# Two hybrid layers on one core: gate steps traced behind the recurrence, and the scheduler's other model of times

## The chip, the cores and the metric

One core of a Trainium2 chip runs the whole program. The metric is the device time of one execution in microseconds (us), the median of several runs. The profile is of one execution more.

## What is computed

Two consecutive layers of a diffusion backbone on 256 context tokens and 256 latent tokens of width 1024. In each layer, cut to what matters:

```
u   = modulate(x)                              # adaLN, one shift and scale per stream
z   = u @ w_in                                 # one combined projection
ys  = [rwkv7(z0), retnet(z1), hgrn2(z2), gqa(z3)]   # four mixers, 256 columns each
m   = sum_i sigmoid(u @ w_gate_i) * (ys[i] @ w_branch_i)
x   = layer_norm(alpha * x + gate1 * (m @ w_out))
x   = layer_norm(alpha * x + gate2 * moe(modulate(x)))   # 16 experts, each picks its tokens, SwiGLU
```

The output is the latent stream after the second layer; layer 1 therefore computes only the 256 latent rows behind its mixers. All is in float32; a product with a weight is made of three products of halves (high x high, high x low, low x high), for which every weight is split into a rounded part and a rest.

## The kernel before

Weights stream from memory once. A layer runs in this order: modulation, input projection, attention, HGRN, RetNet, the RWKV recurrence, the gates, the output projection, the router, and the experts.

**The gates.** For three of the four branches (`wmg`, merged with the branch's weight) there are 8 steps each. A step loads a tile `wr` of 128 x 1280 on SP's queue (`wload`, L238), splits it into `wh` (ScalarE, L183) and `wl` (L211; for all steps of layer 0 and nearly all of layer 1 on POOL, else on VectorE), runs 24 products with u and, after a `yield`, 6 products with the branch's output. For the fourth branch, whose y is RWKV's own output, 8 steps `wg0` run 24 products each (names `m<-mh,wh`, `m<-mh,wl`, `m<-ml,wh` in layer 0, `yh`, `yl`, `y` for `mh`, `ml` in parts of layer 1); `merge_last` (L1325) then makes its 48 branch products. Columns are 512 in layer 0, 256 in layer 1. Buffers of `wr` are 4 in layer 0 and 3 in layer 1, of `wh` and `wl` 2.

**What sets the order.** The program is traced in Python; a list scheduler then walks it with a model of each instruction's time, and gives a free engine the ready instruction that was traced first. So what is traced early has a high priority. `merge_steps` (L1278) is a generator, kept as `self.filler`, and `hook(name)` (L403) traces as many of its half steps as the table `FILL` gives for that place. The recurrence (`rwkv`, L469, with `rwkv_early`, `rwkv_inverse`, `rwkv_late`) calls `hook` after each of its pieces; the keys of these are like `0X0`, `0inv0`, `1W1`, `1f`. Keys that begin with `hl` behind the layer's number, `0hf` and `1hf`, and `1fm` are for other generators (`mods`, `ret_proj`), in attention, HGRN and RetNet. What is left of the generator is traced by `fill()` (L410, called at L1908 in `layer`), behind the recurrence and behind x1, `wout`, `g2` and the router's rows:

```
        self.filler = self.merge_steps(l, lo, u, mg, mgp, yp, ys)
        self.rwkv(l, lo, ys[0], freed)
...
        nc.sync.dma_start(x1, src.rearrange("(t p) d -> p t d", p=P)[:, t0:])
...
        self.fill()
        mh, ml = self.merge_last(l, lo, mg, mgp, ys[0], xs.tile([P, 2, NTOK - lo], F32R, tag="oht", name="yl", bufs=1))
```

**The queues.** SP issues nearly all loads, in the scheduler's order, and each waits at the head of the queue until its buffer is free. When the recurrence's pool is freed by its last product, the loads of x1, `wrt`, `ring` and `first` (experts' weights in 1 MB units) may go; two tiles `rows_in` of `wout` go on POOL's queue (L1893). An expert takes 12 units of 1 MB (`w_e1`, `w_e3`, `w_e2`, four each); the units rotate through the buffers `ring`, `mid`, `low` and `late` (L1548), and the next unit of a buffer can be loaded when PE has read the last one.

Of the kernel before, what the change touches and what calls it, by code (L numbers as in the profile page):

```python
# [50 lines left out]
C_N = C_EVEN + 2  # L51


FILL = {
# [6 lines left out]
}  # L61


def shape_constants():
# [102 lines left out]
class Block:  # L167
# [235 lines left out]
    def hook(self, name):  # L403

        n = FILL.get(f"{self.l}{name}", FILL.get(name, 0))
        work = self.proj if name.startswith("hl") else self.filler
# [1578 lines left out]
```

## Time and profile before

| | us |
|---|---|
| median of 3 runs | 2302.59 |
| lowest, highest | 2302.35, 2312.79 |
| the profiled execution | 2311.96 |
| its span | 2310.2 |
| PE busy in it (89%) | 2048.9 |
| VectorE busy (45%) | 1041.0 |
| ScalarE busy (27%) | 627.2 |
| POOL busy (12%) | 268.1 |

The mean granted clock of the tensor engine is 0.929 of full speed. PE is busy nearly all the time in the mixers of both layers, and the DMA engines nearly all the time among the experts. Of the chain of waits that ended last, PE's work is 63%, transfers 22% and VectorE 10%.

### The profile page before, as it was taken

To read this page: it belongs to the slowest core of one execution; us is meant where nothing else is said; L and a number is where in the kernel's file an instruction comes from. 1 tells how busy PE (TensorE), PEld (TensorE's weight loads), DVE (VectorE), ACT (ScalarE), POOL (GpSimd) and SP (SyncE) were. 2 spreads that over 40 slices of the span, in tenths; PEclk is the share of its full clock that TensorE was granted. 3 is DMA by queue.
4 is the path that set the end of the run, shared out by engine and by line. 5 is a ranking of instruction groups with operands and counts; after the bars stand their busy time and mean duration, and the time that the engine had idled before them with its cause. 6 is when DMAs were issued, how large, how long until landed. Compare 5 with 4: busy or idle time off the path is not lost.

```text
span 2310.2 us, 37585 instructions
## 1 busy us (share of the span) xinstructions
PE 2048.9 (89%) x15964; PEld 1275.7 (55%) x15964; DVE 1041.0 (45%) x2179; ACT 627.2 (27%) x1039; POOL 268.1 (12%) x190
## 2 busy tenths in 40 slices
PE   6999999999999989999999899999889888766775
PEld 3657847677877744333332555868889654222222
DVE  3557755855532536222222557848664642010112
ACT  3353435422222212000000444555343320000000
POOL 2000111233332000000000200103353000000000
PEclk8999999999999989999999899998899988787777
DMA  8354242112124588999999646214222899999996
GB/s 317 97 194 155 64 142 73 41 58 70 56 66 184 201 351 326 422 425 425 426 426 425 220 138 211 69 47 165 92 93 86 338 372 424 424 425 423 424 425 288
DMA packets 96936, 554.85 MB, mean 240 GB/s; under 512 B 11296, under 2 KB 13280, under 8 KB 46848
## 3 DMA queue, kind: packets, MB, share of 16 engines
q1 hardware_dynamic: 95024, 541.83, 60.1%
q0 software_dynamic: 1200, 8.52, 0.9%
q8 instruction: 125, 2.05, 0.3%
q10 hardware_dynamic: 544, 2.10, 0.2%
q14 instruction: 43, 0.35, 0.0%
HBM read 549.13 MB, written 3.28 MB: 239 GB/s over the span
## 4 chain that ended last, share of the span: by engine, by line
PE 63%; DMA 22%; DVE 10%; ACT 2%; issue 2%; POOL 1%; SPq 0%; DVEq 0%; ACTq 0%; POOLq 0%
PE pj L201 14%; PE m L201 13%; PE h L201 12%; PE y L201 9%; DMA late<-in_w_e_dram 8%; PE g L201 6%; DMA mid<-in_w_e_dram 4%; DMA ring<-in_w_e_dram 4%; DMA pair<-in_w_e_dram 3%; PE mod L201 3%; PE w L201 3%; DMA mw<-in_wmod_dram 1%; DMA y<-in_wmod_dram 1%; DVE kb L186 1%; PE w L206 1%
## 5 line engine op out<-in xcount | busy, mean ns | idle before, releaser
L211 POOL TENSOR_TENSOR wl<-wr,wh 128x1280 fp32r<-128x1280 f32 (+1 forms) x62 | 177.7, 2867 | 292.6 <-ACT wh L183 266.2
L183 ACT ACTIVATE wh<-wr 128x1024 fp32r<-128x1024 f32 (+1 forms) x126 | 143.4, 1139 | 190.0 <-PE pj L201 86.4
L201 PE MATMUL m<-mh,wh 128*128 128x512 f32 (+1 forms) x512 | 183.4, 358 | 7.7 <-ACT th L183 7.7
L201 PE MATMUL m<-mh,wl 128*128 128x512 f32 (+1 forms) x512 | 179.4, 350 | 1.0 <-POOL wl L211 1.0
L201 PE MATMUL m<-ml,wh 128*128 128x512 f32 (+1 forms) x512 | 179.0, 350 | 0.0
L201 PE MATMUL h<-late,later 128*32 128x256 f32 (+1 forms) x880 | 143.1, 561 | 28.5 <-DMA late<-in_w_e_dram 28.5
L196 DVE SCALAR_TENSOR_TENSOR h<-h 128x512 f32<-128x512 f32 (+1 forms) x32 | 17.7, 555 | 313.9 <-ACT h L183 313.9
L211 DVE TENSOR_TENSOR wl<-wr,wh 128x1024 fp32r<-128x1024 f32 (+1 forms) x64 | 79.2, 1240 | 109.3 <-ACT wh L183 104.6
L183 ACT ACTIVATE h<-h 128x512 f32<-128x512 f32 (+1 forms) x32 | 15.7, 491 | 401.8 <-PE h L201 401.8
L201 PEld LDWEIGHTS m<-mh,wh 128*128 128x128 f32 x512 | 101.0, 197 | 25.7 <-ACT th L183 9.4
L186 DVE TENSOR_TENSOR h<-h 128x512 f32<-128x512 f32 (+1 forms) x32 | 17.7, 554 | 211.3 <-PE h L201 211.3
L201 PE MATMUL h<-ring,later 128*32 128x256 f32 (+1 forms) x640 | 93.6, 540 | 19.9 <-DMA ring<-in_w_e_dram 19.9
L201 PEld LDWEIGHTS m<-mh,wl 128*128 128x128 f32 x512 | 100.6, 196 | 13.8 <-issue 1.7
L201 PEld LDWEIGHTS h<-late,later 128*32 128x32 f32 (+1 forms) x880 | 45.5, 138 | 112.6 <-issue 63.4
L201 PEld LDWEIGHTS m<-ml,wh 128*128 128x128 f32 x512 | 100.8, 197 | 11.5 <-issue 1.6
L183 ACT ACTIVATE ht<-w 128x512 f32<-128x512 f32 (+1 forms) x32 | 15.7, 491 | 277.4 <-PE w L206 277.4
L201 PE MATMUL y<-late,ht 128*32 128x256 f32 (+1 forms) x536 | 73.5, 501 | 9.5 <-DMA late<-in_w_e_dram 6.9
L201 PE MATMUL h<-mid,later 128*64 128x512 f32 (+1 forms) x352 | 65.6, 569 | 9.0 <-DMA mid<-in_w_e_dram 9.0
L201 PEld LDWEIGHTS h<-ring,later 128*32 128x32 f32 (+1 forms) x640 | 30.1, 136 | 74.1 <-DMA ring<-in_w_e_dram 33.5
L201 PE MATMUL y<-ring,ht 128*32 128x256 f32 (+1 forms) x448 | 62.3, 526 | 9.7 <-DMA ring<-in_w_e_dram 6.3
L183 ACT ACTIVATE th<-m 128x512 f32<-128x512 f32 (+1 forms) x50 | 24.6, 492 | 164.6 <-PE m L201 164.6
L201 PE MATMUL pj<-mh,wl 128*128 128x512 f32 x152 | 61.9, 407 | 0.0
(629 smaller groups left out, 4480.5 us busy)
## 6 DMA issues: line engine op xcount, KB each, us to landing
late<-in_w_e_dram SPq DMA_DIRECT2D x144, 1024.0 KB, 19.5
ring<-in_w_e_dram SPq DMA_DIRECT2D x109, 1024.0 KB, 19.7
mid<-in_w_e_dram SPq DMA_DIRECT2D x63, 1024.0 KB, 19.7
pair<-in_w_e_dram SPq DMA_DIRECT2D x36, 1024.0 KB, 19.6
wr<-in_wmg_dram SPq DMA_DIRECT2D x48, 640.0 KB, 3.9
mw<-in_wmod_dram SPq DMA_DIRECT2D x48, 512.0 KB, 5.0
y<-in_wmod_dram SPq DMA_DIRECT2D x48, 512.0 KB, 4.0
low<-in_w_e_dram SPq DMA_DIRECT2D x20, 1024.0 KB, 19.8
```

Source lines behind the costliest of these rows:

```text
L183: self.nc.scalar.activation(out=out, in_=in_, func=func, **kw)
L186: self.nc.vector.tensor_tensor(out, a, b, op)
L196: self.nc.vector.scalar_tensor_tensor(out, a, s, b, op0, op1)
L201: self.nc.tensor.matmul(out, lhsT, rhs, start=start, stop=stop)
L206: self.nc.tensor.transpose(out, in_, self.ident[b:b + n, b:b + n])
L211: (eng or self.nc.vector).tensor_tensor(lo, src, hi.bitcast(F32), ALU.subtract)
```

## The change

Two edits. The table loses every key of the recurrence's hooks, so that `hook` traces no gate there and all 32 steps of a layer are traced by `fill()`, with the lowest priority of what can run then. And the tile context schedules with its other model of times. No instruction and no arithmetic is added or removed. Behind the table the changed kernel's line numbers are lower by 7.

```diff
-FILL = {
-    "0hf": 2, "0X0": 2, "0inv0": 1, "0W0": 3, "0R0": 3, "0Y0": 2, "0X1": 1, "0inv1": 1, "0W1": 2, "0R1":
...
+FILL = {'0hf': 2, '0hl00': 1, '0hl02': 1, '0hl04': 1, '0hl10': 3, '0hl12': 2, '0hl16': 1, '1hf': 2, '1hl00': 1, '1hl04': 1, '1hl06': 1, '1hl12': 1, '1hl16': 3, '1hl18': 3, '1hl11': 1, '1fm': 1, '0hl18': 2, '1hl15': 1, '1hl13': 1}
...
-    with tile.TileContext(nc) as tc:
+    with tile.TileContext(nc, schedule_with_timeline_sim=True) as tc:
```

On PE, runs of 24 to 96 gate products stood in the recurrence of layer 0 at the hooked places, and 186 products (merge_last's 48 among them) behind the router's product `wrr`. Now many short runs stand in the recurrence, 90 products between the transposes of `rx` and `wrr` (44 before), and 390 behind it. In layer 1 the last run grows from 62 to 240. The second HGRN scan of layer 0 has 54 projection products of 512 columns between its steps, where 86 stood.

POOL in layer 0, from the recurrence's second half to the gates' end (`wl` is a split, `ktm` and `tmp` belong to the recurrence, `y` is its last sum, `rows_in` is `wout`). Before:

```order
L703 MEMSET tmp 128x256
L704 MEMSET tmp 128x16
L211 TENSOR_TENSOR wl<-wr,wh 128x1280 x7
L646 TENSOR_TENSOR kb_3579<-kb_3579,ec 128x512 x2
L211 TENSOR_TENSOR wl<-wr,wh 128x1280
L764 MEMSET ktm 32x16x32 x2
L211 TENSOR_TENSOR wl<-wr,wh 128x1280 x8
L211 TENSOR_TENSOR wl<-wr,wh 128x1024 x2
L551 TENSOR_TENSOR y_114<-y_114,bo_5791 128x512
L551 TENSOR_TENSOR y_114<-y_114,bo_5799 128x512
L1893 DMA rows_in<-in_wout_dram 128x2048 x2
L211 TENSOR_TENSOR wl<-wr,wh 128x1024 x6
```

The same piece with the change:

```order
L696 MEMSET tmp 128x256
L697 MEMSET tmp 128x16
L204 TENSOR_TENSOR wl<-wr,wh 128x1280 x3
L639 TENSOR_TENSOR kb_3454<-kb_3454,ec 128x512 x2
L204 TENSOR_TENSOR wl<-wr,wh 128x1280
L757 MEMSET ktm 32x16x32 x2
L204 TENSOR_TENSOR wl<-wr,wh 128x1280 x8
L544 TENSOR_TENSOR y_114<-y_114,bo_4811 128x512
L544 TENSOR_TENSOR y_114<-y_114,bo_4819 128x512
L1886 DMA rows_in<-in_wout_dram 128x2048 x2
L204 TENSOR_TENSOR wl<-wr,wh 128x1280 x6
L204 TENSOR_TENSOR wl<-wr,wh 128x1024 x8
```

Behind the recurrence's last sum 6 splits stood, and now 14; in layer 1 it was 1, and is 10. Of the 62 splits on POOL 38 are left ahead of these sums.

SP in layer 1, at the end of the gates (`wg` are the g0 steps, `wb` the last branch's weight). Before:

```order
L242 DMA wr<-in_wmg_dram 128x1280 x24
L242 DMA wr<-in_wg_dram 128x1024 x7
L530 DMA g_14065<-in_g_dram 128x256
L242 DMA wr<-in_wg_dram 128x1024
L242 DMA wr<-in_wb_dram 128x1024 x2
L1896 DMA x_14196<-xd 128x2x1024
L1904 DMA wrt<-in_wrt_dram 128x128
L1569 DMA ring_14766<-in_w_e_dram 128x2048
L1569 DMA ring_14768<-in_w_e_dram 128x2048
L1569 DMA ring_14770<-in_w_e_dram 128x2048
L1569 DMA first<-in_w_e_dram 128x2048 x3
```

The same piece with the change:

```order
L235 DMA wr<-in_wmg_dram 128x1280 x4
L235 DMA wr<-in_wg_dram 128x1024
L1889 DMA x_13046<-xd 128x2x1024
L1897 DMA wrt<-in_wrt_dram 128x128
L1562 DMA ring_14766<-in_w_e_dram 128x2048
L1562 DMA ring_14768<-in_w_e_dram 128x2048
L1562 DMA ring_14770<-in_w_e_dram 128x2048
L235 DMA wr<-in_wg_dram 128x1024
L1562 DMA first<-in_w_e_dram 128x2048 x3
L235 DMA wr<-in_wg_dram 128x1024 x6
L235 DMA wr<-in_wb_dram 128x1024 x2
```

Seven of the eight loads of g0 weights have moved behind x, and six of them behind the first expert units too. In layer 0 the last two of the 24 `wmg` loads and all eight of g0 stand behind x, two rings and first.

SP among the experts of layer 0, some 18 units after the first reload. Before:

```order
L1569 DMA late_7270<-in_w_e_dram 128x2048
L1569 DMA late_7272<-in_w_e_dram 128x2048
L1569 DMA ring_7274<-in_w_e_dram 128x2048
L1569 DMA ring_7276<-in_w_e_dram 128x2048
L1569 DMA ring_7278<-in_w_e_dram 128x2048
L1569 DMA mid_7280<-in_w_e_dram 128x2048
L1569 DMA mid_7282<-in_w_e_dram 128x2048
L1569 DMA mid_7284<-in_w_e_dram 128x2048
L1569 DMA mid_7286<-in_w_e_dram 128x2048
L1569 DMA low_7288<-in_w_e_dram 128x2048
L1569 DMA late_7290<-in_w_e_dram 128x2048
```

The same piece with the change:

```order
L1562 DMA late_7270<-in_w_e_dram 128x2048
L1562 DMA mid_7280<-in_w_e_dram 128x2048
L1562 DMA mid_7282<-in_w_e_dram 128x2048
L1562 DMA mid_7284<-in_w_e_dram 128x2048
L1562 DMA mid_7286<-in_w_e_dram 128x2048
L1562 DMA low_7288<-in_w_e_dram 128x2048
L1562 DMA late_7290<-in_w_e_dram 128x2048
L1562 DMA late_7272<-in_w_e_dram 128x2048
L1562 DMA ring_7274<-in_w_e_dram 128x2048
L1562 DMA ring_7276<-in_w_e_dram 128x2048
L1562 DMA ring_7278<-in_w_e_dram 128x2048
```

Six units that were behind a late and three ring units have gone ahead of them. Such exchanges go on for some five experts of layer 0 and for three of layer 1; the order behind them is the old one.

## Rows read from the trace of the kernel before

**Rows 1.** Page, slices: GB/s moved in 40 equal slices of the span.

```profile
GB/s 317 97 194 155 64 142 73 41 58 70 56 66 184 201 351 326 422 425 425 426 426 425 220 138 211 69 47 165 92 93 86 338 372 424 424 425 423 424 425 288
```

**Rows 2.** Windows, recurrence of layer 0: engines busy (instructions), PE clock, DMA share, GB/s.

```profile
430.00:480.00 50.00, 45.45 (x563) 35.36 (x561) 37.82 (x85) 22.22 (x40) 13.35 (x6) 1.00 0.17 54
480.00:560.00 80.00, 79.29 (x925) 65.13 (x929) 36.77 (x50) 17.18 (x20) 25.95 (x11) 0.98 0.21 67
560.00:640.00 80.00, 76.62 (x1048) 63.11 (x1040) 46.85 (x79) 23.64 (x33) 23.98 (x11) 0.98 0.17 56
640.00:700.00 60.00, 58.31 (x458) 41.68 (x453) 20.13 (x34) 21.19 (x29) 17.44 (x9) 1.00 0.30 104
```

**Rows 3.** Windows, layer 1's recurrence, the same columns.

```profile
1570.00:1600.00 30.00, 25.76 (x250) 22.12 (x249) 27.12 (x61) 14.53 (x30) 12.77 (x9) 0.83 0.57 227
1600.00:1660.00 60.00, 53.19 (x782) 47.79 (x783) 45.04 (x100) 26.07 (x47) 22.45 (x12) 0.88 0.26 88
1660.00:1700.00 40.00, 36.52 (x582) 33.25 (x583) 32.52 (x66) 10.68 (x17) 11.41 (x5) 0.92 0.16 51
1700.00:1760.00 60.00, 56.84 (x1046) 54.09 (x1044) 29.34 (x47) 20.06 (x30) 29.84 (x12) 1.00 0.31 101
```

**Rows 4.** Timeline of PE, end of layer 0's gates: start, us, instruction, idle before.

```profile
691.37 1.98 PE L201 MATMUL w<-rows,ident 128*128 128x512 f32 x4 [1.69 <-ACT g L183]
...
699.75 0.39 PE L201 MATMUL m<-ml,wh 128*128 128x512 f32 x1
699.98 0.39 PE L201 MATMUL m<-mh,wl 128*128 128x512 f32 x1
704.35 0.66 PE L201 MATMUL w<-wrr,one 128*128 128x64 f32 x2 [3.98 <-DVE wrr L1443]
...
705.34 0.63 PE L201 MATMUL m<-ml,wh 128*128 128x512 f32 x1
705.77 0.63 PE L201 MATMUL m<-mh,wl 128*128 128x512 f32 x1
```

**Rows 5.** Timeline of PE, layer 1: gate products, and their end.

```profile
1753.57 0.28 PE L201 MATMUL m<-yh,wl 128*128 128x256 f32 x1
1753.68 0.28 PE L201 MATMUL m<-yh,wh 128*128 128x256 f32 x1
...
1796.37 2.93 PE L201 MATMUL w<-rows,ident 128*128 128x512 f32 x3 [2.48 <-ACT g L183]
```

**Rows 6.** Timeline of SP's queue: x1 in layer 0 and in layer 1.

```profile
688.70 0.38 SPq L1896 DMA_DIRECT2D x<-in_xt_dram  x1
...
1790.92 0.39 SPq L1896 DMA_DIRECT2D x<-xd  x1
```

**Rows 7.** Timeline of VectorE: an ordinary operation, and three that meet a split.

```profile
394.09 3.05 DVE L186 TENSOR_TENSOR z<-zp 128x512 f32<-128x512 f32 x1 [3.46 <-ACT zp L183]
...
438.22 0.22 DVE L186 TENSOR_TENSOR tmp<-tmp 128x60 f32<-128x60 f32 x1
...
439.21 2.37 DVE L186 TENSOR_TENSOR tmp<-tmp 128x63 f32<-128x63 f32 x1
...
1791.20 4.40 DVE L186 TENSOR_TENSOR y<-y,gt 128x256 f32<-128x256 f32 x2 [2.98 <-POOL y L551]
```

**Rows 8.** Timeline of POOL: one of the splits.

```profile
438.50 3.01 POOL L211 TENSOR_TENSOR wl<-wr,wh 128x1280 fp32r<-128x1280 f32 x1 [9.58 <-ACT wh L183]
```

**Rows 9.** Windows, HGRN and RetNet of layer 0, columns as in rows 2.

```profile
215.00:375.00 160.00, 155.80 (x928) 108.27 (x928) 100.41 (x222) 71.96 (x112) 18.28 (x23) 1.00 0.27 85
```

**Rows 10.** Windows, the experts of layer 0, columns as in rows 2.

```profile
834.00:870.00 36.00, 35.23 (x166) 12.42 (x163) 4.18 (x8) 3.59 (x8) 0.00 (x0) 1.00 0.94 373
870.00:900.00 30.00, 30.00 (x168) 18.12 (x166) 25.96 (x52) 10.63 (x23) 0.00 (x0) 1.00 0.75 286
900.00:940.00 40.00, 38.44 (x177) 13.44 (x178) 10.98 (x22) 2.10 (x4) 0.00 (x0) 1.00 0.97 381
...
1000.00:1250.00 250.00, 235.86 (x1060) 81.58 (x1062) 66.46 (x127) 16.63 (x28) 0.12 (x1) 1.00 1.01 425
```

More of the change, by code (lines that the diff above doesn't have):

```diff
@@ L51 @@
 C_N = C_EVEN + 2
-FILL = {
[6 rows of a table removed]
-}
+FILL = {'0hf': 2, '0hl00': 1, '0hl02': 1, '0hl04': 1, '0hl10': 3, '0hl12': 2, '0hl16': 1, '1hf': 2, '1hl00': 1, '1hl04': 1, '1hl06': 1, '1hl12': 1, '1hl16': 3, '1hl18': 3, '1hl11': 1, '1fm': 1, '0hl18': 2, '1hl15': 1, '1hl13': 1}
 def shape_constants():
```

5 rows, old and new, of the table FILL are left out of this document.

## The prediction

> **What bounds the kernel now.** I read the utilisation slices first, then busy time by stretch, the timelines of the places that the order moves, and at last the two streams of loads. The slices show two regimes in each layer. From about the 17th slice (920 us) to the 22nd, and from the 34th to the last but one, the DMA engines move 422 to 426 GB/s; these are the experts, and the loads alone set their length [rows 1]. In the other slices the transfers run far below that, and PE does the work of the mixers and the gates. So a change of order can gain in three ways only: PE waits less among the mixers, PE gets more of its clock there, or the experts' loads start or run with fewer holes.
>
> Layer 0, 430 to 700 us, is the RWKV recurrence with gates around it. PE is busy 45.45, 79.29, 76.62 and 58.31 of 50, 80, 80 and 60 us [rows 2], which leaves 10.3 us of waits, with a granted clock of 0.98 to 1.0. The same stage of layer 1, 1570 to 1760 us, has busy times of 25.76, 53.19, 36.52 and 56.84 in 30, 60, 40 and 60 us, so 17.7 us of waits, and clocks of 0.83, 0.88, 0.92 and 1.00 [rows 3]. If the time of a stretch goes with its clock, the loss there is 30 x 0.17 + 60 x 0.12 + 40 x 0.08 = 15.5 us. In all 28 us of waits and 15.5 us of clock are the most that this stage can give back.
>
> **What one gate costs.** Column blocks of 512 start 0.23 us apart in layer 0 [rows 4], of 256 0.11 to 0.12 us apart in layer 1 [rows 5]. A step of 30 such products is 6.8 or 3.5 us of PE. None is added or removed, so the gates' own PE time is at nothing; what counts is what they stand in front of, and what PE meets where they no longer stand.
>
> **The change, term by term.**
>
> (a) *Layer 0, the end of the gates.* Before, the last branch's rows are split, the router's weight arrives late, and PE waits 1.69 us for g and 3.98 us for wrr [rows 4]. After the second wait the gate products show 0.63 us instead of 0.39 for their length and start 0.43 us apart [rows 4]; 13 of them run so, which is 13 x 0.2 = 2.6 us. In the new order 90 gate products (20 us) instead of 44 stand between the transposes of rx and wrr, while x is issued at 688.70 us and wrr was ready at 704.35, 15.7 us later [rows 4, 6]. The cover is long enough; I take all three away: -8 us. The next thing that can be late there is the gate weights, two of which now stand behind 9 MB of x, wout, ring and first; but six steps are loaded already, 41 us, and 9 MB at 425 GB/s are 21 us. So nothing is added.
>
> (b) *Layer 1, the same place.* Before, all gate weights are issued ahead of x (1790.92 us) and the rings behind it [rows 6], and PE waits 2.48 us for g [rows 5]. After, seven of the eight g0 loads stand behind x, the three rings and, six of them, behind first too; with wout on POOL's queue that is again 9 MB, 21 us at 425 GB/s, before six of the steps can run. PE has four steps and one more, 144 products of 0.12 us, or 17 us, and some 4 us of small products. With the load's own time and the split the third g0 step comes some 8 us late, and the others follow at their own pace. Bounds: 0, if the buffers come free earlier than I think, and +21, if nothing covers it. I take +8 less the 2.5: +6 us.
>
> (c) *The recurrence itself.* Three effects. First, the scheduler now puts gates only where its other model sees PE idle, instead of in fixed runs of up to 90 products. Where a fixed run held up a chain, the chain gets shorter, and waits of the place after it go. I take half of the 28 us and a third of the 15.5 us: -14 and -5. Second, the cover shrinks: 204 products leave the recurrence of layer 0 (46 us) and 178 that of layer 1 (21 us) for the end. Where the model's chain is shorter than the real one, PE now meets the next product of the recurrence too early. The model cannot be expected to hold this: the POOL split wl of 438.50 us lasts 3.01 us, and the vector operation of 439.21 us that meets it takes 2.37 us, where one of 0.22 us with almost the same shape stands a little ahead [rows 7, 8]. Over the trace 27 vector operations that run beside the 62 splits are so stretched, from 394.09 us (3.05 us) to the last pair at 1791.20 us (4.40 us for the two) [rows 7], by 2.1 us on average. Third, 17 of the splits move out of the recurrence (8 in layer 0, 9 in layer 1), with 17 x 27/62 x 2.1 = 16 us of such stretching; but PE hid most of it behind gates, so I take nothing for it. The 38 splits that stay stretch 38 x 27/62 x 2.1 = 35 us; I take that half of it is now uncovered: +16. The sum is -3, between -44 (all waits and clock back, nothing uncovered) and +35.
>
> The Trainium skill (SBUF — State Buffer, the part "Who interferes with whom") says of this that VectorE and GpSimd share one pair of ports, that it is an exclusive lock and that the loser blocks for the whole instruction. The trace agrees [rows 7, 8], since the stretched operation ends 0.1 us from the end of the split. By that rule alone, all 38 splits would cost up to their full length wherever the vector engine is on the path, which speaks against the change; the 27 of 62 measured say that most find it idle or on its other port.
>
> (d) *The mixers ahead of it.* The other model also re-sorts attention, HGRN and RetNet. PE is busy 155.80 of 160 us there [rows 9], so little can be won. In the new order the second HGRN scan is covered by some 54 projection products instead of 86; 32 x 0.23 = 7 us less. Some waits for modulation weights may go in exchange. Bounds: -4 (all idle time of this stretch) and +14 (7 us in either of two scans). I take +6.
>
> (e) *The experts' loads, layer 0.* Between 834 and 940 us the stream has holes: 373, 286 and 381 GB/s against 425 after 1000 us [rows 10], so 36 x 52/425 + 30 x 139/425 + 40 x 44/425 = 18 us. The loads go in a fixed order and wait for late, ring and so on to be read. The new order puts six loads whose buffers come free early (mid, low, late) ahead of four that wait, from which 6 x 2.47 us (1 MB at 425 GB/s) = 15 us of work could fill the hole of 870 to 900 us, 10 us long. PE is busy 235.86 of 250 us in that stage and must keep up, so I take -7, between 0 and -15. In layer 1 the first loads stand as before: nothing.
>
> The sum is -8 + 6 - 3 + 6 - 7 = -6 us. The profiled execution took 2311.96 us, 9.4 above the median of 2302.59. On the median it is 2302.6 - 6 = 2296.6; on the profiled execution it would be about 2306.
>
> **The rivals.**
>
> *Slower, by uncovered stretching and just-in-time gates.* In the place of (c)'s -3 stands +30: no waits come back and nearly all 35 us show. This decides if PE waits at products of the recurrence (gm, ktm, lr) and not at gates. 2296.6 + 33 = 2330. For it: 46 us of cover leave layer 0. Against it: the splits stretch vector operations today too, and layer 0 has no more than 10.3 us of waits [rows 2].
>
> *Faster: waits and clock come back.* (c) gives -30 and (b) costs nothing beyond its -2.5: 2296.6 - 27 - 6 = 2264. For it: low clocks in layer 1 stand exactly where waits are frequent [rows 3]. Against it: every stage is full of PE work already, above 95% in layer 0.
>
> *The burst of loads holds the gates in both layers.* +21 in place of nothing in (a) and of +8 in (b): 2296.6 + 34 = 2331. It decides if SP reaches x before the steps ahead of it have been loaded. Against it stand the six loaded steps.
>
> *Nothing moves the end.* The experts' loads take the same time whenever they start; if PE ends the mixers when it did, the time stays at 2303. This is inside my forecast's own range.
>
> **How the numbers follow.** I give the forecast 0.44 (own range 2284 to 2312), the faster case 0.27, the slower one 0.20 and the burst 0.09. A measurement of this kernel can tell about 0.5%, 11.5 us, from no change. Of the forecast 0.11 lies below 2291, 0.30 between, 0.03 above 2314; the faster case lies all below; of the slower and the burst 0.04 falls inside. That makes 0.38 faster, 0.34 the same, 0.28 slower. For 8 in 10 the range reaches from 2258, a little under the faster case, to 2334, a little over the two slow ones.
>
> **What would show it.** Right: no wait for wrr near the end of layer 0's gates and full clock behind it; a wait for a g0 weight of 5 to 10 us at layer 1's end; in the 30 us that begin 36 us after layer 0's first reload, over 350 GB/s; vector operations beside wl still at 2 to 3 us, and waits of PE in the recurrence between 20 and 35 us in all. Wrong: waits of PE for kb, gm or lr above 45 us, or a layer 1 clock of 1.0 from 1570 us on.

## The result: 1.2% slower, and the profile after

The changed kernel takes 2335.09 us (median of 4 runs, 2332.14 to 2336.57), the kernel before in the same comparison 2303.68 us. The ratio is 1.0124, with a 95% interval of 1.0101 to 1.0148: 31 us are lost on the medians and 29 by the ratio, where 6 were forecast to be won. The profiled execution took 2334.0 us. That of before lies 8 us above its median, so the two spans differ by 22.0 us only; all sums below are made on the spans. Executions in a slow state are left out of all numbers here, among them a second profile of the kernel before (2624.6 us, mean granted clock 0.724), so each kernel has one profile.

The page of the changed kernel: span, busy time of the engines, and the granted clock and GB/s in 40 slices.

```profile
span 2332.2 us, 37564 instructions
...
PE 2047.6 (88%) x15964; PEld 1290.5 (55%) x15964; DVE 1034.4 (44%) x2179; ACT 623.4 (27%) x1039; POOL 272.1 (12%) x190
...
PEclk9999979899999989999999999888899888777887
GB/s 337 127 152 140 151 53 65 36 47 37 60 236 64 199 345 396 384 426 425 426 425 421 205 168 175 55 68 131 57 59 267 205 349 423 424 425 424 423 424 285
```

PE has the same 15964 products and the same busy time within 1.3 us. The mean clock fell from 0.929 to 0.921. The stream of the experts looks as in [rows 1], only later.

I cut both traces at the same products: the first `ar,kb` product of the recurrence, the first product with `oh` (the output projection), the first and the last product of the experts. For each stretch three numbers are worked out: its length, PE's idle time in it, and (1 - mean granted clock) x length as lost clock. An idle time counts with the product that ends it. The last two show where time went, but their sum is no exact account of it: not all work goes with the clock, and the same small products can fill more or less of PE's busy time (an example stands under (c) below).

| length (idle, lost clock), us | before | after |
|---|---|---|
| layer 0 ahead of the recurrence | 407.3 (29.5, 8.5) | 447.6 (34.7, 32.4) |
| layer 0, recurrence and gates | 346.7 (18.3, 10.2) | 320.5 (11.4, 6.8) |
| layer 0, output projection and router | 78.0 (12.6, 8.5) | 74.6 (10.9, 6.8) |
| layer 0, experts | 455.5 | 448.7 |
| layer 1 ahead of the recurrence | 293.2 (16.6, 8.5) | 308.0 (21.6, 27.3) |
| layer 1, recurrence and gates | 239.4 (21.6, 17.2) | 241.9 (29.2, 17.4) |
| layer 1, output projection and router | 48.9 | 48.9 |
| layer 1, experts | 430.5 | 431.1 |

The first two lengths of a layer together went from 754.0 to 768.1 us in layer 0, and from 532.6 to 549.9 in layer 1. Little work has moved over the line between them: ahead of the first `ar,kb` PE has the same products as before, but for 28 gate products more in layer 0 (6.4 us at 0.23 us each) and 14 fewer in layer 1 (1.7 us at 0.12). With these taken into account the stretch ahead of the recurrence is 33.9 us longer in layer 0 and 16.5 in layer 1, together 50 us, and the recurrence with the gates 19.8 us shorter in layer 0 and 0.8 longer in layer 1. So what was lost stands **ahead of the recurrence**: idle time and lost clock rise there from 38.0 to 67.1 us in layer 0 and from 25.1 to 48.9 in layer 1, and four fifths of that is clock.

The profiles of the experiments repeat this. Two of them (the table alone, and layer 0's keys) have the order of before on PE ahead of layer 0's recurrence, product for product, and take 403.7 and 408.2 us there; two (the model alone, and gates at the longest chains) have that of the changed kernel, and take 441.8 and 442.2 us.

The place in layer 0 is plain in the windows from HGRN's scans to the start of the recurrence. First the kernel before (columns as in rows 2: engines busy, with instructions, PE's clock, DMA share, GB/s):

```profile
290.00:320.00 30.00, 28.27 (x170) 17.30 (x170) 15.66 (x37) 8.54 (x17) 6.31 (x7) 1.00 0.42 129
320.00:340.00 20.00, 20.00 (x81) 7.68 (x73) 9.57 (x22) 9.39 (x14) 0.10 (x1) 1.00 0.52 171
340.00:360.00 20.00, 20.00 (x85) 10.35 (x85) 12.92 (x26) 11.46 (x17) 1.98 (x3) 1.00 0.18 53
...
420.00:450.00 30.00, 29.64 (x346) 23.00 (x343) 26.04 (x62) 13.89 (x24) 6.29 (x5) 0.89 0.07 23
```

The same windows of the changed kernel:

```profile
290.00:320.00 30.00, 28.53 (x160) 19.14 (x160) 22.66 (x50) 9.35 (x12) 5.66 (x5) 1.00 0.29 89
320.00:340.00 20.00, 16.43 (x62) 11.77 (x64) 7.88 (x23) 4.97 (x13) 1.45 (x2) 0.55 0.09 26
340.00:360.00 20.00, 19.18 (x55) 8.49 (x52) 7.18 (x17) 7.09 (x11) 0.35 (x4) 0.68 0.05 14
...
420.00:450.00 30.00, 27.64 (x110) 20.50 (x109) 14.99 (x37) 13.64 (x24) 4.59 (x4) 0.72 0.07 23
```

From 320 to 360 us the clock is 0.55 and 0.68 of full speed, near its lower level of 1.2 GHz, where before it was 1.00 throughout. A second place is the norm of `kk`, right ahead of the recurrence (the last row of the changed kernel, 0.72; the last row of before lies in its recurrence already, which begins at 407.3 us). PE's timeline of the changed kernel shows what runs there (start, us, instruction, idle before and what ended it):

```profile
321.68 1.22 PE L194 MATMUL g<-e 64*128 64x128 f32 x5 [2.59 <-DVE e L179]
...
325.25 1.62 PE L194 MATMUL g<-e 64*128 64x128 f32 x6 [0.69 <-DVE e L179]
...
338.51 2.82 PE L194 MATMUL y<-ac,hi 128*64 128x512 f32 x5 [0.69 <-ACT ac L176]
```

These are the last steps of HGRN's second scan (`g<-e`) and its outputs, and no projection product stands between them. I call a product of the projections, the modulation or the gates *cover*, since it doesn't wait for the chain beside it. From 315.9 to 356.1 us PE has no cover at all, only 125 products of HGRN and RetNet; before, no such stretch behind attention is longer than 10 us in either layer. Layer 1 shows the same at HGRN's end. Before, and then after:

```profile
1470.00:1500.00 30.00, 29.04 (x221) 24.50 (x221) 22.55 (x62) 15.08 (x28) 4.05 (x7) 1.00 0.18 54
1500.00:1530.00 30.00, 29.71 (x133) 17.40 (x130) 14.26 (x33) 15.78 (x26) 0.35 (x4) 1.00 0.20 62
```

```profile
1470.00:1500.00 30.00, 26.64 (x151) 21.20 (x151) 18.23 (x50) 14.90 (x26) 3.81 (x6) 0.89 0.18 57
1500.00:1530.00 30.00, 25.34 (x100) 15.53 (x100) 13.16 (x39) 10.58 (x21) 3.04 (x7) 0.66 0.13 43
```

The order of PE's instructions tells why. Counted are the products with projection weights that are issued from the start of the program:

| projection products issued | before | after |
|---|---|---|
| up to attention's last product, layer 0 | 173 | 480 |
| up to HGRN's first `al,hi` product, layer 0 | 575 | 720 |
| up to its last | 758 | 768 |
| from the first to the last, layer 0 | 183 | 48 |
| the same in layer 1 | 147 | 48 |
| behind the norm of `kk` (last `cst,kk` product), up to the recurrence, layer 0 | 118 | 0 |
| the same in layer 1 | 135 | 0 |

The other model puts projection products into attention, whose last product moves from 131.3 to 213.0 us, and has few left where HGRN's scans end, and none behind the norm of `kk`. Of the modulation products (128 up to the recurrence of layer 0) 16 stood behind the last `al,hi` product before, and now none (the profile shows each as two).

### The profile page after: what moved, and what is told of

It reads as the page before. It is cut to its first block, busy times and chain, and to the rows that moved or that the text cites. A ratio compares the mean times of both kernels' runs of the same rounds, so it can differ in the third digit from the quotient of the medians.

```text
span 2332.2 us, 37564 instructions
## 1 busy us (share of the span) xinstructions
PE 2047.6 (88%) x15964; PEld 1290.5 (55%) x15964; DVE 1034.4 (44%) x2179; ACT 623.4 (27%) x1039; POOL 272.1 (12%) x190
## 4 chain that ended last, share of the span: by engine, by line
PE 51%; DMA 33%; DVE 11%; ACT 3%; issue 2%; SPq 0%; POOL 0%; DVEq 0%; POOLq 0%; ACTq 0%
PE pj L194 14%; PE m L194 11%; DMA late<-in_w_e_dram 11%; DMA mid<-in_w_e_dram 8%; PE h L194 7%; PE y L194 6%; PE g L194 6%; DMA ring<-in_w_e_dram 4%; DMA pair<-in_w_e_dram 3%; PE mod L194 3%; DMA mw<-in_wmod_dram 2%; PE w L194 2%; DVE tmp L179 1%; DMA y<-in_wmod_dram 1%; DMA wr<-in_wg_dram 1%
## 5 line engine op out<-in xcount | busy, mean ns | idle before, releaser
L194 PE MATMUL h<-late,later 128*32 128x256 f32 (+1 forms) x880 | 128.3, 531 | 34.5 <-DMA late<-in_w_e_dram 34.5
L194 PE MATMUL h<-ring,later 128*32 128x256 f32 (+1 forms) x640 | 84.9, 521 | 27.5 <-DMA ring<-in_w_e_dram 27.5
L194 PE MATMUL y<-late,ht 128*32 128x256 f32 (+1 forms) x536 | 73.0, 491 | 11.9 <-DMA late<-in_w_e_dram 9.4
L194 PE MATMUL pj<-mh,wh 128*128 128x512 f32 x152 | 62.9, 414 | 0.0
L189 DVE SCALAR_TENSOR_TENSOR ht<-y,gt,g 128x512 f32<-128x512 f32 (+1 forms) x32 | 18.3, 612 | 99.0 <-PE y L194 98.9
## 6 DMA issues: line engine op xcount, KB each, us to landing
low<-in_w_e_dram SPq DMA_DIRECT2D x20, 1024.0 KB, 19.8
```

Source lines behind the costliest of these rows:

```text
L189: self.nc.vector.scalar_tensor_tensor(out, a, s, b, op0, op1)
L194: self.nc.tensor.matmul(out, lhsT, rhs, start=start, stop=stop)
```

## The experiments

The theory that came out of these traces: the loss is cover that HGRN's end and the norms have no longer. Its rivals were the one of the prediction (gates just in time, vector operations stretched by POOL's splits) and the table.

**Table or model.** Two runs undo one edit each; the first has the new table and the model of before, the second the table of before and the other model.

```diff
-    with tile.TileContext(nc, schedule_with_timeline_sim=True) as tc:
+    with tile.TileContext(nc) as tc:
```

> Table without the recurrence's keys, scheduler with its old model. Up to the recurrence of layer 0 the order of PE is that of before, row for row; then the old model leaves 752 gate products of layer 0 and 587 of layer 1 behind the recurrence, where the change left 390 and 240. If the loss of the change comes from the lost gates beside the recurrence (theory T), this kernel loses far more than the change: 362 products of 0.23 us and 347 of 0.12 us, 83 and 42 us, of cover less, about 2400 us or more. If it comes from the re-sorted mixers ahead of the recurrence (theory M), this kernel is near before, under 2320 us. Experts of layer 0 as long as before (455 us from their first product to their last), since their loads have the old order.

> Table of before, scheduler with the other model. Theory T: the gates' runs of before stand in the recurrence, so its waits are those of before and the time is near 2304 us less the 7 us that the experts' loads gained, 2290 to 2305. Theory M: the first mixers of layer 0 are those of the change (clock of 0.8 from 300 to 375 us), which costs 12 to 15 us in layer 0 and something in layer 1: 2315 to 2335. Both: experts of layer 0 7 us shorter than before.

Table alone: 1.0063 [1.0041, 1.0086], 2315.69 us. Model alone: 1.0145 [1.0091, 1.02], 2331.89 us (three executions). So the model alone gives the whole loss, and the table costs something that can be measured only under the first model. With the model alone idle time and lost clock ahead of the recurrence are 61.8 and 50.9 us; with the table alone 34.3 and 26.7, as before, and the loss stands in layer 1's recurrence (idle 32.7 us where 21.6 stood).

**Whose keys.** The model and table of before, without the keys of layer 0's recurrence.

```diff
-    "0hf": 2, "0X0": 2, "0inv0": 1, "0W0": 3, "0R0": 3, "0Y0": 2, ...
+    "0hf": 2, ...
```

> Old model; the keys of the recurrence taken out for layer 0 alone. With both layers' keys out the time rose by 14 us, and in its profile layer 0's mixers were not longer than before (waits 50.6 against 47.8) and layer 1's waits longer by 12.6 us. If the keys matter in layer 1 alone, this kernel is within 5 us of before (2298 to 2308); if layer 0's cover matters as well, 2309 to 2318.

1.0002 [0.9979, 1.0026], 2303.9 us. Layer 0's hand-placed gates are worth nothing that can be measured; with the run above, the 0.6% of the table are layer 1's keys. A gate step is only 3.5 us of cover there instead of 6.8, which may be why; it wasn't tried.

**Stretched vector operations.** In the changed kernel all gate splits move from POOL to VectorE.

```diff
-                h, lw = self.wsplit(self.wload(self.a["wmg"][l, i - 1, d]), self.nc.gpsimd if ... else None)
+                h, lw = self.wsplit(self.wload(self.a["wmg"][l, i - 1, d]))
...
-            h, lw = self.wsplit(self.wload(self.a["wg0"][l, d]), self.nc.gpsimd)
+            h, lw = self.wsplit(self.wload(self.a["wg0"][l, d]))
```

> The change, with all splits of gate weights on VectorE instead of POOL. Rival S says that uncovered stretching of vector operations beside POOL's splits (58 us in all, 26 operations) makes the loss: then the time falls by 10 to 25 us, to 2310 to 2325. Theory T and M: the 62 operations of 1.24 us (77 us) load VectorE more and the time stays or rises, 2330 to 2350.

1.0132 [1.0097, 1.0168], 2330.67 us, so no gain. The page's groups of the changed kernel, and then of this run (busy time and mean ns of one, idle before):

```profile
L204 POOL TENSOR_TENSOR wl<-wr,wh 128x1280 fp32r<-128x1280 f32 (+1 forms) x62 | 177.4, 2863 | 321.9 <-ACT wh L176 311.4
...
L204 DVE TENSOR_TENSOR wl<-wr,wh 128x1024 fp32r<-128x1024 f32 (+1 forms) x64 | 80.2, 1257 | 147.1 <-ACT wh L176 147.0
```

```profile
L204 DVE TENSOR_TENSOR wl<-wr,wh 128x1024 fp32r<-128x1024 f32 (+1 forms) x126 | 169.1, 1345 | 130.6 <-ACT wh L176 129.5
```

POOL's 62 splits are gone; VectorE does all 126, which are 89 us more of its time. Of VectorE's operations 40 took over 0.6 us more than the quicker ones of their kind in the changed kernel (71.7 us in excess); 14 do here (13.7 us). The time is that of the changed kernel, and so, nearly, are idle time and lost clock ahead of the recurrence (35.1 and 29.0 us in layer 0). Could VectorE's added work hide a gain elsewhere? In the recurrence of layer 1, where it might show, idle time and lost clock fall from 46.6 to 34.2 us, and in that of layer 0 they rise from 18.2 to 28.5. So some of it may cancel, but the loss ahead of the recurrence is none of it, and the rival of the prediction, which put the loss in the recurrence, falls.

**Gates at the longest chains.** The changed kernel with one gate step traced at each piece of the inverse and some more (`0inv0`, `0inv1`, `1inv0`, `1inv1`, `0V1`, `1V0`).

```diff
-FILL = {'0hf': 2, ...
+FILL = {'0inv0': 1, '0inv1': 1, '1inv0': 2, '1inv1': 2, '0V1': 1, '1V0': 1, '0hf': 2, ...
```

> The change, with the keys of the inverse (inv) and of the piece ahead of it (V) back in the table. In layer 1 this puts some 20 gate products more between the parts of the inverse, where PE waited 6.9 and 5.9 us; in layer 0 the order stays as it was. Theory T: these two waits fall to under 2 us each, the time by 5 to 12 us, to 2323 to 2330. Theory M: nothing moves by more than 3 us.

1.0158 [1.0118, 1.0198], 2336.27 us: no gain. This run is no clean test, though. Of the two waits the second fell from 5.94 to 2.11 us, but at the place of the first PE waits 8.25 us at a gate product that the new keys put there, for `th` of ScalarE. That gates in the recurrence are not what is missing rests on the run with the model alone, which has all of them.

**Cover moved to HGRN's end.** The changed kernel with the keys of HGRN's hooks set later.

```diff
-'0hl00': 1, '0hl02': 1, '0hl04': 1, '0hl10': 3, '0hl12': 2, '0hl16': 1, ...
+'0hl00': 1, '0hl04': 1, '0hl10': 1, '0hl12': 1, '0hl13': 1, '0hl14': 1, '0hl15': 1, '0hl16': 1, ...
```

> The change, with RetNet's projections pulled later by the HGRN scan (one at each of the levels 2 to 6 of its second half, instead of three at the first), which puts 48 products of 0.23 us among the last three levels of layer 0, where PE had HGRN's own small products alone. Theory M': the new model believes the scan to be shorter than it is, spends the projections early, and leaves the scan's end bare; waits and half clock there are the loss. Then ahead of the recurrence the loss of waits and clock falls by 8 to 15 us in layer 0 and 3 to 10 in layer 1, and the time to 2312 to 2325. Rival R: the clock falls for another reason in that stretch (the kk norm, or RetNet's mixing interleaved with projections): 2330 to 2340.

1.0089 [1.0054, 1.0125], 2326.21 us: some 8 us less by the ratio, but the intervals of this run and of the changed kernel overlap, and it is outside both ranges that I gave. In layer 0 idle time and lost clock ahead of the recurrence are 59.9 us, where the order of the changed kernel gave 61.7 to 67.1 in its three profiles; in layer 1 about 48, as there. Windows of this run:

```profile
290.00:320.00 30.00, 25.86 (x143) 17.90 (x144) 20.62 (x51) 7.26 (x10) 4.23 (x5) 0.83 0.23 69
320.00:340.00 20.00, 19.12 (x98) 12.84 (x96) 10.11 (x21) 8.28 (x17) 1.33 (x4) 1.00 0.18 53
340.00:360.00 20.00, 19.38 (x67) 10.49 (x68) 10.02 (x22) 8.98 (x14) 0.31 (x3) 0.91 0.05 14
```

The bare place at 320 us is mended, with a clock of 1.00, and a new one has come up ahead of it, at 290 to 320 us with 0.83.

**The next bare place.** The statistic of kk's norm takes the modulation's PSUM bank instead of the one that it shares with RetNet, first with the late keys, then in the kernel before.

```diff
-for p, rs in enumerate(self.rstd(kk, 512, self.bone, self.eps12, pz, ...)):
+for p, rs in enumerate(self.rstd(kk, 512, self.bone, self.eps12, pz, ..., "mod")):
```

> The change with the late pulls, and the norm of kk ahead of the recurrence in the PSUM bank that the modulation leaves free, instead of the bank of RetNet's mixing. In the order its small products (cst,kk and ident,rx) then stand among RetNet's products and projections, where before they stood alone. Theory M': this stretch (420 to 440 us in layer 0, clock 0.54 and 0.61; 1580 to 1600 in layer 1, 0.73 and 0.75) is the second bare place; the loss of waits and clock there, about 11 us in layer 0 and 8 in layer 1, falls by half or more: 2326 less 8 to 14, 2312 to 2318. Rival R: the clock falls for what stands behind it (start of the recurrence), and the time stays at 2322 to 2330.

> The kernel before with the same bank for kk's norm, and nothing else. Before, 109 projection products stood behind this norm and covered it, so that only about 3 us of waits and 3 to 5 us of clock were lost there in both layers together. Theory M': a gain of 0 to 5 us, 2298 to 2304. If it gains over 8 us, the norm cost more than its stretch showed.

1.0086 [1.0053, 1.0118], 2329.52 us, and 0.9997 [0.9978, 1.0015], 2305.39 us. Nothing comes of it in either. With the late keys that is what the rival says: the bare place moves to the start of the recurrence (420 to 450 us: PE busy 23.07 of 30 us, clock 0.73).

**More cover held back.** With the late keys, the weights of two projection blocks are loaded early into `mg`'s memory, so that 72 of their products are free to stand at the start of the recurrence; the second run adds the bank.

```diff
+            w = room
+            self.nc.sync.dma_start(w, src)
...
+        self.shift_block(l, b, ..., pz, zz, None if i is None else self.mg[:, 2 * i:2 * i + 2].rearrange("p k c -> p (k c)"))
```

> The change with the late pulls (2326 us), and the weights of the recurrence's last two large projections loaded into mg's memory, which RetNet frees, so that the new model cannot spend them inside RetNet's mixing: in the order 72 products then stand behind the kk norm and the first products of the recurrence, as 109 did before. Theory M'': the start of the recurrence is bare since the projections that covered it were spent early; then its waits and clock (420 to 450 us, 1580 to 1610 us) lose 5 to 12 us less in both layers together, 2314 to 2321. Rival R'': RetNet's second half becomes bare instead and takes it back: 2322 to 2332.

> The same with the kk norm in the modulation's bank, so that its small products run inside RetNet's mixing, and the 72 products stand right at the recurrence's start. Theory M'': both places covered, 3 to 8 us below the kernel with the hold alone, 2308 to 2318. Rival R'': no more than 3 us from it.

1.0161 [1.0129, 1.0192], 2343.65 us, and 1.0125 [1.0085, 1.0164], 2336.67 us (three executions). The first is slower than with the late keys alone; for the second the intervals overlap. The first lies above both ranges that I gave. The second is 7 us below the first, as I had said, but far above its range of 2308 to 2318. Windows of the first show where the products are missing, in RetNet's second half and its norms:

```profile
360.00:400.00 40.00, 34.94 (x121) 18.27 (x120) 16.14 (x27) 15.69 (x25) 1.57 (x4) 0.96 0.09 31
400.00:420.00 20.00, 15.97 (x63) 12.91 (x63) 6.29 (x9) 7.34 (x11) 1.28 (x1) 0.66 0.14 53
420.00:450.00 30.00, 29.50 (x138) 22.82 (x136) 21.20 (x38) 14.30 (x23) 9.40 (x6) 1.00 0.24 81
```

The start of the recurrence is mended (29.50 of 30 us, 1.00), at the cost of the place ahead of it, where the run of the late keys had 40.00 of 40 us (360 to 400 us): from 379.6 to 413.7 us there is no cover now. So in these runs the products act as one stock: what covers one place with them bares another.

**The same loss without the other model.** Up to here the theory was held up by traces alone: what was moved under the other model never gave back more than some 8 us. Two last runs come from the other side. They keep the model and the gate keys of before and only use the cover early: in the first RetNet's projections, to the very counts of the changed kernel (720 ahead of HGRN's first `al,hi` product), in the second the modulation products too, by a hook in attention.

```diff
-    "0hl00": 1, "0hl02": 1, "0hl04": 1, "0hl10": 3, "0hl12": 2, "0hl16": 1, ... "0hl18": 2, ...
+    '0hl00': 6, '0hl10': 1, '0hl14': 1, '1hl00': 5, '1hl10': 1, '1hl14': 1
...
+                    self.hook("at")
```

The last line, with the keys `'0at': 1, '1at': 1`, is in the second run only.

> The kernel before, with its own model and its own gate keys; only the hooks of HGRN's scans are placed anew, so that RetNet's projections are used up early: 720 projection products are issued ahead of the first al,hi product of layer 0 and 2568 ahead of that of layer 1, the same counts as in the changed kernel (before: 575 and 2437), and 48 and 42 instead of 183 and 147 are left beside the scans. Theory 1 (the loss of the other model is cover that HGRN's end and RetNet's norms no longer have): the scans show half-clock stretches in both layers, and the time is 15 to 35 us longer, 2318 to 2340 us, ratio 1.006 to 1.015, with waits and lost clock ahead of the recurrence up from 38 and 25 us by at least 10 us in each layer. Rival (the loss comes from how attention is laid out under the other model, not from what is left for HGRN): within 0.3% of before, and that sum within 6 us of before's in both layers.

> The run w4 with one more hook: in attention one step of the modulation generator is traced behind each query tile, so that all 128 and 192 modulation products stand ahead of HGRN's first al,hi product, too (before: 96 and 192; the changed kernel: 110 and 192). Theory 1: the second half of HGRN and RetNet's norms in layer 0 have no modulation products left beside them either, so another 4 to 12 us on top of w4; ratio 1.008 to 1.020. Rival: within 0.3% of before, as w4. If w4 shows the loss and this adds nothing, RetNet's projections are the cover that counts and the modulation products are not.

1.0098 [1.0076, 1.012], 2327.74 us, and 1.0202 [1.0179, 1.0225], 2351.26 us. Ahead of the recurrence:

| length (idle, lost clock), us | layer 0 | layer 1 |
|---|---|---|
| before | 407.3 (29.5, 8.5) | 293.2 (16.6, 8.5) |
| projections early | 418.1 (32.6, 11.9) | 303.9 (23.2, 15.4) |
| modulation products, too | 436.5 (33.2, 30.7) | 304.9 (23.6, 15.4) |
| the changed kernel | 447.6 (34.7, 32.4) | 308.0 (21.6, 27.3) |

Windows of the second run in layer 0:

```profile
240.00:290.00 50.00, 45.20 (x298) 39.45 (x298) 39.53 (x92) 17.79 (x29) 4.22 (x5) 0.87 0.19 55
290.00:320.00 30.00, 28.36 (x130) 20.60 (x128) 16.14 (x38) 14.34 (x22) 3.33 (x4) 0.71 0.04 16
320.00:340.00 20.00, 16.87 (x115) 13.81 (x114) 19.23 (x47) 7.50 (x8) 4.09 (x5) 0.95 0.09 27
340.00:360.00 20.00, 18.98 (x63) 9.67 (x61) 5.01 (x13) 8.41 (x19) 0.24 (x3) 0.67 0.11 39
```

The place of before that had a clock of 1.00 is at 0.67 now, with HGRN's outputs alone on PE. So an order that spends the cover early costs time under the first model as well, 23 and 47 us on the medians, and it does so ahead of the recurrence, which itself is untouched (its two stretches keep 342 to 346 and 238 to 243 us). The kind of the loss is shown by this; its size in the changed kernel only in part, for there the stretches ahead of the two recurrences grew by 50 us, and here by 22 and 41.

Counts alone don't explain the difference. In layer 0 the first run has those of the changed kernel: 720 and 768 projection products up to the first and the last `al,hi`, 108 modulation products instead of 110 up to the first, and none behind the last. Yet idle time and lost clock rise by 6.5 us there instead of 29.1. What differs is how the cover is spread. These are all stretches of over 10 us without cover, from attention's end to the recurrence, and how much of each ran at half clock:

| length (of it at half clock), us | layer 0 | layer 1 |
|---|---|---|
| before | none | none |
| the changed kernel | 40.2 (30.7), 11.9 (9.5) | 14.0 (6.8), 27.8 (21.2) |
| late keys | 11.2 (8.3), 20.3 (3.4), 11.7 (8.8) | 21.4 (13.7), 19.1 (14.8), 10.8 (7.7) |
| projections early | 24.6 (6.8) | 25.8 (13.7) |
| modulation products, too | 38.3 (27.6), 34.2 (17.1) | 22.5 (10.2) |

The first run's bare stretch in layer 0 is 25 us long, the changed kernel's 40; and these two runs leave the norm of `kk` its 118 projection products, where the changed kernel has none and a second bare stretch. In layer 0 the second run goes further than the changed kernel: all 128 modulation products stand ahead of the first `al,hi`.

Two sizes I missed. The projections alone cost layer 0 less in idle time and clock than the 10 us I had set (6.5), and layer 1 more (13.5). The modulation products cost 23.5 us on the medians where I had expected 4 to 12; ahead of layer 0's recurrence they weigh more than the projections (19.4 against 6.5 us of idle time and clock).

No version here is faster than the kernel before; the one with layer 0's keys removed and the one with kk's bank equal it.

## Why the prediction was wrong

The sum was -6 us, and the measured one is +31 on the medians, +22 on the spans. Term by term, on the spans:

**(d), the mixers ahead of the recurrence, is the step that failed.** It stood at +6 with bounds of -4 and +14; measured it is +50, 33.9 us in layer 0 and 16.5 in layer 1. Several things were wrong in it. I counted 54 instead of 86 products in the second scan of layer 0 and multiplied the difference by their own time, as if only idle time could be lost. I took "PE is busy 155.80 of 160 us, so little can be won" [rows 9] as if it also said that little could be lost; a stretch that is full because of its cover can lose most. I left the clock out: the same row has 1.00, and in the changed kernel two of its windows have 0.55 and 0.68, for 20 us each that is 9.0 + 6.4 = 15 us, more than the whole bound. Nor did the working follow the products up to where they had gone, 480 instead of 173 ahead of attention's end. And no row of it is from layer 1.

**(a) Layer 0's gate end, -8: right, about -7.** The waits of [rows 4] for g and wrr and the half clock behind them are gone: the product with wrr runs at 676.51 us with no idle time before it, and PE is busy all of the 50 us of gates from 700 us on, at full clock. One new wait stands there, 1.51 us at 675.00 us for a gate's `th`. **(e) The experts' loads, -7: right**, 455.5 to 448.7 us. The first reload is at 844.75 us instead of 833.91, so the windows of [rows 10] are set 11 us later: the stream moves 401, 425 and 351 GB/s in them, where it moved 373, 286 and 381. The hole is filled, as forecast, and a smaller one stands behind it. Windows of the changed kernel:

```profile
700.00:750.00 50.00, 50.00 (x223) 41.38 (x222) 6.21 (x7) 14.78 (x20) 21.58 (x9) 1.00 0.24 74
845.00:881.00 36.00, 36.00 (x172) 13.18 (x170) 4.09 (x8) 3.12 (x7) 0.00 (x0) 1.00 0.99 401
881.00:911.00 30.00, 30.00 (x140) 14.76 (x138) 10.30 (x21) 8.19 (x18) 0.00 (x0) 1.00 1.01 425
911.00:951.00 40.00, 40.00 (x210) 17.93 (x206) 26.90 (x53) 4.78 (x8) 0.00 (x0) 1.00 0.90 351
```

**(b) Layer 1's gate end, +6: right in kind.** PE waits for the splits of late g0 weights, where it waited 2.48 us for g [rows 5]. Its timeline:

```profile
1800.96 0.39 PE L194 MATMUL m<-mh,wl 128*128 128x256 f32 x1 [1.92 <-POOL wl L204]
...
1807.70 0.58 PE L194 MATMUL m<-mh,wh 128*128 128x256 f32 x1 [3.84 <-ACT wh L176]
1808.08 0.42 PE L194 MATMUL m<-ml,wh 128*128 128x256 f32 x1
1808.95 0.58 PE L194 MATMUL m<-mh,wh 128*128 128x256 f32 x1 [0.45 <-ACT wh L176]
```

With 0.68 us at 1818 us these make 6.9 us, so +4.4. Behind the split is the load, as forecast: ScalarE's `wh` of 1806.59 us had itself waited 2.31 us for `wr`.

**(c) The recurrence, -3: mis-sized, about -17.** Windows of the changed kernel to set beside [rows 2, 3], some 20 us later in layer 0 and 30 in layer 1:

```profile
450.00:500.00 50.00, 44.25 (x692) 36.11 (x691) 46.74 (x106) 22.74 (x45) 12.43 (x7) 0.90 0.09 28
500.00:560.00 60.00, 58.43 (x840) 48.64 (x839) 38.45 (x65) 14.55 (x23) 14.69 (x8) 0.97 0.17 52
560.00:640.00 80.00, 77.96 (x1216) 61.97 (x1216) 42.01 (x80) 19.38 (x27) 19.49 (x8) 1.00 0.17 57
640.00:700.00 60.00, 58.17 (x261) 46.45 (x260) 23.16 (x32) 24.43 (x31) 27.79 (x12) 1.00 0.59 229
...
1600.00:1630.00 30.00, 25.16 (x279) 23.04 (x277) 27.60 (x40) 13.71 (x26) 15.85 (x7) 0.89 0.27 88
1630.00:1690.00 60.00, 52.03 (x1019) 47.47 (x1017) 45.91 (x112) 20.85 (x38) 15.55 (x10) 0.89 0.17 57
1690.00:1730.00 40.00, 34.06 (x770) 32.16 (x768) 31.73 (x63) 14.73 (x24) 14.21 (x7) 0.91 0.19 60
1730.00:1790.00 60.00, 58.87 (x755) 53.39 (x752) 35.05 (x60) 24.36 (x37) 31.44 (x14) 1.00 0.43 160
```

The waits are 11.2 + 19.9 = 31 us, inside the 20 to 35 that I gave, where before they were 28. In layer 1 two long ones stand out, on PE's timeline of the changed kernel, where the longest wait of that stretch was under 3 us before:

```profile
1652.57 1.64 PE L194 MATMUL g<-lr,tv 32*32 32x16 f32 x108 [6.86 <-ACT tv L176]
...
1710.09 1.62 PE L194 MATMUL g<-tmp,gm 32*32 32x32 f32 x105 [5.94 <-DVE tmp L713]
```

The lengths say more than the waits. With (a), (b) and the moved gate products taken out, the recurrence with its gates is some 13 us shorter in layer 0 (19.8 less 6.8) and 4 in layer 1 (0.8 less 4.4): -17 in all, inside the bounds of -44 and +35, but far from -3. Idle time and lost clock show part of it, in layer 0 28.5 to 18.2 us with (a) in it. Another part is in PE's busy time, where I had not looked: the 2398 products of that stretch of layer 0 that are no gate products fill 85.0 us of it instead of 94.8.

Both halves of my working that cancelled were wrong. Half the waits did not come back, and the +16 for stretched operations found no place: 26 operations beside the splits are still stretched, by 58 us in all as before, and the run without POOL's splits takes as long.

The Trainium skill (SBUF — State Buffer, "Who interferes with whom") calls the port pair that VectorE and GpSimd share an exclusive lock; that the loser is blocked for the whole instruction it says of VectorE's two-port modes, and of an operation with two SBUF inputs that it contends with GpSimd's reads. The trace agrees on the single operation [rows 7, 8], which ends with the split; the run with all splits on VectorE did not get shorter by taking it away.

In layer 0 the output projection and router are 3.4 us shorter, which I had not forecast, and layer 1's experts 0.6 longer. The terms are then -7 for (a), +4 for (b), -17 for (c), +50 for (d), -7 for (e), and these two: +22 together, the difference of the spans. Where the forecast had (a), (b), (c) and (e) at -12, they make some -26; so a second error, in (c), hid part of that in (d). The profiled execution of before is a long one, and the 9 us by which the medians differ more belong to no term. A stretch varies by some 5 us between profiles of one order (above), so (c) and (d) are rough to that extent.

**The rivals.** The slower one gave 2330 us, and that is near the measured time, by another mechanism: its waits were to stand in the recurrence, which in layer 0 got better, and its price was to be the stretching, whose removal gained nothing. The burst holds the gates in layer 1 only. Nothing came near the faster one (its own terms give 2261 and not 2264, since (b) goes from +6 to -2.5). No case of mine held a loss ahead of the recurrence of more than 14 us.

Two things stay open: why the other model keeps attention's chain so long that it fills it with projections, since no run here changed that model's times; and whether the cover could be spread under it without loss, since every run that tried bared another place.

## What to carry to other kernels

Independent products are a stock that covers serial chains, and a scheduler that spends it at the first chain leaves the last ones bare; before a change of order, count how much of it is left at each chain that must be covered, up to the end of the stage, and how long the longest stretch without any is. A stretch in which PE is 97% busy can lose far more than its 3%: bound a loss there by what its cover does, idle time and clock together. And separate the edits first: here the table looked like the change and the model's one word was the loss.

## What the runs showed of the hardware

The clock can fall where PE is hardly idle. These are windows inside the changed kernel's stretch without cover, and the one behind it, where projections stand again:

```profile
322.00:342.00 20.00, 18.11 (x69) 12.13 (x68) 5.92 (x17) 4.96 (x13) 1.45 (x2) 0.50 0.00 1
346.00:356.00 10.00, 9.87 (x16) 2.79 (x16) 4.54 (x13) 3.67 (x7) 0.21 (x2) 0.50 0.09 28
356.00:380.00 24.00, 24.00 (x91) 14.89 (x89) 11.76 (x18) 12.51 (x19) 0.21 (x2) 1.00 0.16 49
```

From 346 to 356 us PE is busy 9.87 of 10 us, and the granted clock is 0.50, its level of 1.2 GHz; the longest single wait of the whole stretch is 2.59 us. From 356 us on it is 1.00. In the kernel before nearly the same products of HGRN, with cover of 512 columns between them, run at 1.00. So the busy time on the page doesn't tell a stretch that keeps its clock from one that doesn't; the row of the clock does.

The Trainium skill (TensorE: Matmul & The Clock Gate, "A second HAM failure mode: psum-queue depth-cycling") tells of a kernel in which frequent short idle spells between groups of products, not a long wait for a transfer, make the clock swing between its two levels. The trace agrees with the kind of it: no wait in this stretch is for a DMA. The kernel that the Trainium skill tells of cycles through PSUM banks; no run here shows whether that plays a part.
